# A hybrid SSM and attention layer on one core: VectorE's order up to the scan, with the tables of C A^d built last

## The chip, the cores and the metric

One core of a Trainium2 chip runs the whole layer in one launch. The time is device microseconds from the start to the end of the program, as the median of several runs. The engines meant below are TensorE (PE, with its weight loads PEld), VectorE (DVE), ScalarE (ACT), GpSimd (POOL) and SyncE (SP), whose queue issues nearly all DMAs. Each works through its own list of instructions in order; an instruction that waits on a semaphore holds up all that stand behind it on its engine.

## The reference

One layer of a decoder, in float32, for 1024 positions of 1024 features. What the change touches lies in the first sub-layer, up to the state scan:

```python
mod = (silu(c) @ w_mod + b_mod)                  # sh1, sc1, g1, sh2, sc2, g2
h = _rms(x, norm1_w) * (1 + sc1) + sh1
proj = h @ w_in                                  # u (512) | q (512) | k (128) | v (128)
# S5: 32 groups of 16 channels, each driving a complex state of 64
a = exp(dt * lam); bb = f * (b_re + i b_im)      # zero-order hold
bu = einsum("blgh,gph->blgp", u, bb)
s[t] = a * s[t-1] + bu[t]                        # associative scan over the 1024 positions
y = Re(C s) + D u; z = gelu(y); out = z * sigmoid(z @ w_glu + b_glu)
# beside it: sliding-window attention (128) with sinks on q, k, v; then per-branch norms,
# w_out and the gate g1; then the channel sub-layer: norm, w_up, conv of width 3, silu gate, w_down
```

## The kernel before

A scheduler puts the instructions of each engine in an order when the program is built; the code gives it dependences and priorities. `tc.issue_after(i)` makes what stands inside it come after instruction i in that order. Tiles with one name share one place in SBUF: a new tile of a name may be written once all readers of the old one are done. All products that must be exact run as three products of rounded halves (`mm3`), each half made by a ScalarE cast and a VectorE subtraction (`split`).

**Load stage.** For eight blocks of 128 features, x, one column block of w_mod and the weights of u come in. VectorE makes a column of sc1 (`emit_mod`, L178: a product of 128x1024 with a running sum), scales and splits x into `hT`, and TensorE adds to six banks for u (positions j, j+8, ... for j = 0 to 5) and, through a matrix of ones, the sums of squares in banks 6 and 7. `rsqrt_mean` (L187) makes `rstd` of these, with two ScalarE and two VectorE steps for each half. Then the eight numbers that scale u (`rc`) are turned by TensorE, and the products for j = 6 (in bank 6) and j = 7 (in bank 0) follow.

**Shift.** Eight more `emit_mod` make the columns of sh1 (L291 to L293) from 512 KB blocks that pass through three places. `shs` holds them rounded, `shift_u` (L299) multiplies them with the weights of u on TensorE, and VectorE reduces that to `Bu`.

**Tables.** From A^0 to A^8 (`PWr`, `PWi`) the helper `outer` makes, on VectorE, four tables `IB` of B A^d (128x1024, 8 steps of d) and five tables `CAt` of C A^d (128x1008 and 128x576, 9 steps). Each table takes two products and a sum.

**Up to the scan.** Positions go in 128 chunks of 8. U (in the place S16) is transposed by TensorE, four groups to a bank, and ScalarE adds Bu on the way out (`emit_ut`); the tables IB are transposed too (`emit_wj`, ScalarE copies). Three banks (4, 5, 6) take turns for both. Their product gives what each chunk adds to the states; ScalarE copies it to SR and SI, which lie in S16 as well, so that their first writers (two memsets, L578 and L579) wait until U is transposed. `h0` is a generator that puts the products for the key, value and query heads between these steps; inside `pe.pin(True)` TensorE's order is as written.

**Scan.** `cmac` works up and down six levels on VectorE, through a bank (`bk7`) for the products; eight instructions for each half of the first level, one dependent on the other. The columns of the heads are normed between them. After the scan the halves of SR and SI are exchanged (ScalarE, VectorE, ScalarE), and TensorE makes y with the tables CA; gelu, GLU and attention follow.

Of the kernel before, what the change touches and what calls it, by code (L numbers as in the profile page):

```python
# [14 lines left out]
ADD, SUB, MUL, MAX, MIN = ALU.add, ALU.subtract, ALU.mult, ALU.max, ALU.min  # L15

L = 1024
D = 1024
# [44 lines left out]
def hymba_kernel(ctx, tc, xT, c, wmod, wu, wkvq, small, consts, relb, pq, wglu, wout, wup, wdn, out):  # L63
# [7 lines left out]
    def new(tag, dt=F32):  # L71
        return pool.tile([128, SIZES.get(tag, 1024)], dt, tag=tag, name="t" + tag)
# [44 lines left out]
    def tt(eng, o, a, b, op):  # L117
        return eng.tensor_tensor(out=o, in0=a, in1=b, op=op)  # L118
# [7 lines left out]
    def stt(o, a, s, b, op0, op1):  # L126
        return vec.scalar_tensor_tensor(out=o, in0=a, scalar=s, in1=b, op0=op0, op1=op1)  # L127
# [41 lines left out]
    cact = new("X7")  # L169
# [17 lines left out]
    def rsqrt_mean(o, t_, ps, n):  # L187

        act.activation(out=o, in_=ps, func=AF.Abs_reciprocal_sqrt, scale=1.0 / n, bias=eps)
        act.activation(out=t_, in_=o, func=AF.Square, scale=math.sqrt(0.5 / n))  # L190
        stt(t_, ps, n * 1e-6, t_, ADD, MUL)
        stt(o, t_, -1.5, o, ADD, MUL)

    ab, na = [0], [3]

# [71 lines left out]
    rtmp = new("A11")  # L267
    for h in range(2):
        hs = slice(h * 512, h * 512 + 512)
        rsqrt_mean(rstd[:, hs], rtmp[:, hs], bank[6 + h], D)  # L270
    for j in range(T):
        pe.matmul(bank[7][:, j:j + 1], rstd[0:1, j:1024:T], ones[0:1, 0:1], start=True, stop=True)
    act.copy(rc, bank[7][:, 0:8])
# [14 lines left out]
        u_out(j, b)  # L288


    mst = [new("X4"), new("X5"), new("A9")]  # L291
    for k in range(8):
        emit_mod(k, mst[k % 3], cact)  # L293
    shs = pool.tile([128, 16], F32R, name="shs")
    shr = RT(shs.rearrange("p (k s) -> p k s", s=2))
    act.copy(shr.r[:, :, 0], mod[:, 0:8])
# [2 lines left out]
    def shift_u():  # L299
        b = mbank()  # L300
        for k in range(8):
            s_ = [shs[:, 2 * k + i:2 * k + i + 1].to_broadcast([128, 128]) for i in range(2)]
            pe.matmul(b, s_[0], wus[k][0].r, start=(k == 0), stop=False)
            pe.matmul(b, s_[0], wus[k][1].r, start=False, stop=False)
            pe.matmul(b, s_[1], wus[k][0].r, start=False, stop=(k == 7))
        tmp = new("A11")[:, 0:512]
        tt(vec, gh(tmp), gh(b), S("mod16").rearrange("p (o h) -> p o h", o=1).to_broadcast([128, 32, 16]), MUL)
        vec.tensor_reduce(out=Bu, in_=gh(tmp), axis=mybir.AxisListType.X, op=ADD)

# [105 lines left out]
    def outer(eng, o, tmp, g0, ng, nd, u, v):  # L415
        o = o.rearrange("p (g d h) -> p g d h", d=nd, h=16)
        tmp = tmp.rearrange("p (g d h) -> p g d h", d=nd, h=16)
        shp = [128, ng, nd, 16]

        def bx(w_):  # L420
            return gh(w_)[:, g0:g0 + ng, :].rearrange("p g (o h) -> p g o h", o=1).to_broadcast(shp)

        def by(w_):
            return w_[:, g0:g0 + ng, 0:nd].rearrange("p g (d o) -> p g d o", o=1).to_broadcast(shp)

        tt(eng, o, bx(u), by(PWr), MUL)
        tt(eng, tmp, bx(v), by(PWi), MUL)
        tt(eng, o, o, tmp, ADD)

    IB = [new(f"A{5 + i}") for i in range(4)]  # L430
    hp = ctx.enter_context(ExitStack())
    hp.enter_context(tc.high_priority(0))
    for i in range(4):
        tmp = new("A10") if i == 3 else IB[i + 1]
        outer(vec, IB[i], tmp, 8 * i, 8, 8, Bb, Bsw)
    hp.close()
    CAt = [new(f"A{i}") for i in range(5)]
    for i in range(4):
        outer(vec, CAt[i][:, 0:1008], CAt[i + 1][:, 0:1008], 7 * i, 7, 9, P1, P2)
    for q in range(2):  # L440
        outer(vec, CAt[4][:, q * 288:(q + 1) * 288], CAt[4][:, 600:888], 28 + 2 * q, 2, 9, P1, P2)

    def CA(g):
        return CAt[g // 7][:, (g % 7) * 144:(g % 7 + 1) * 144]


    sA, sB = new("X4"), new("X5")
# [90 lines left out]

    def emit_ut(i):
        if i % 2 == 0:  # L540
            UTt[i // 2] = new(f"A{5 + i // 2}")
        b = abank()
        for q in range(4):
            g = 4 * i + q
            pe.transpose(b[:, q * 128:(q + 1) * 128], U[:, g * 128:(g + 1) * 128], ident)
        for q in range(4):
            g = 4 * i + q
            act.activation(out=UTt[i // 2][:, (g % 8) * 128:(g % 8 + 1) * 128], in_=b[:, q * 128:(q + 1) * 128], func=AF.Identity, bias=Bu[:, g:g + 1])

    for i0, n_ in ((0, 4), (4, 2), (6, 2)):  # L550
        for i in range(i0, i0 + n_):
            emit_wj(i)
        for i in range(i0, i0 + n_):
            emit_ut(i)

    def UT(g):
        return UTt[g // 8][:, (g % 8) * 128:(g % 8 + 1) * 128]
# [7 lines left out]
    for i in range(4):  # L565
        br_, bi_ = abank(), abank()
        for q in range(4):
            for par in range(2):
                g = 2 * (4 * i + q) + par
                ps = slice(par * 64, par * 64 + 64)  # L570
                pe.matmul(br_[ps, q * 128:(q + 1) * 128], WJ(g)[:, 0:64], UT(g), start=True, stop=True)
                pe.matmul(bi_[ps, q * 128:(q + 1) * 128], WJ(g)[:, 64:128], UT(g), start=True, stop=True)
        next(h0)
        evac(SR[:, 4 * i:4 * i + 4, 1:129], br_.rearrange("p (g c) -> p g c", c=128), "I")
        if i != 1:
            next(h0)
        evac(SI[:, 4 * i:4 * i + 4, 1:129], bi_.rearrange("p (g c) -> p g c", c=128), "I")
    vec.memset(SR[:, :, 0:1], 0.0)  # L578
    vec.memset(SI[:, :, 0:1], 0.0)  # L579

    pst.close()


    em, mid = new("A9"), new("A10")
# [780 lines left out]
```

## Time and profile before

| | |
|---|---|
| median of 3 runs | 1137.26 us (1137.13 to 1140.05) |
| the profiled execution | 1138.01 us |
| its span in the trace | 1136.1 us |
| TensorE busy | 92% |
| VectorE busy | 82% |
| ScalarE busy | 51% |
| GpSimd busy | 24% |
| mean granted clock of TensorE | 0.962 |

The span leaves out some 1.9 us of the execution around it. A busy share is a mean over stages with different limits, so the stage from the load to the scan is read by itself, from the order of instructions in time and from what ended each wait. Times in rows are us from the span's start. A row of a timeline gives the start, the busy time of the whole group, the engine, the line, the operation, what it writes and reads, and the count; busy times of neighbours overlap a little, so that the distance from start to start is the step.

### The profile page before, as it was taken

Reading aid. Unit: us, or ns where it says so; the run is one execution under the profiler, and the core shown is the slowest. Engines: PE = TensorE matmul, PEld = TensorE weight load, DVE = VectorE, ACT = ScalarE, POOL = GpSimd, SP = SyncE. Lnnn points to the kernel's source line nnn. Section 1 sums busy time; section 2 is a strip of 40 time slices with the busy share of each in tenths; the row PEclk is TensorE's granted clock in tenths of the full one; section 3 lists DMA queues with packets and bytes.
Section 4 is the critical chain, followed back from the end, with each engine's and each line's share of the span. In section 5 each row is a group of like instructions: output and inputs, shape, how many; then the busy total and the mean of one; then the engine's idle time right before and its main releaser. Section 6 shows DMA issues by size and latency. Waiting matters only on the chain.

```text
span 1136.1 us, 13319 instructions
## 1 busy us (share of the span) xinstructions
PE 1050.8 (92%) x4692; PEld 828.1 (73%) x4692; DVE 928.0 (82%) x1493; ACT 581.0 (51%) x1008; POOL 269.0 (24%) x153
## 2 busy tenths in 40 slices
PE   6989999579989899779999999999999979989998
PEld 4877777366556577657888888888888768768876
DVE  7994899949887587888777878797778797998985
ACT  5415443578895366736544545455444554434342
POOL 0000000011233102762222223212212143353541
PEclk9989999689999899979999999999999989999999
DMA  9501516014018855222223232423123359220002
GB/s 364 224 19 38 118 50 93 1 66 139 19 47 213 258 180 155 93 93 94 92 86 112 82 128 93 154 88 112 56 93 116 125 210 382 74 93 1 1 38 112
DMA packets 48487, 128.14 MB, mean 113 GB/s; under 512 B 6146, under 2 KB 14114, under 8 KB 48419
## 3 DMA queue, kind: packets, MB, share of 16 engines
q1 hardware_dynamic: 46114, 123.09, 31.8%
q0 software_dynamic: 2304, 4.20, 2.3%
q8 instruction: 37, 0.61, 0.2%
q14 instruction: 32, 0.25, 0.1%
HBM read 105.28 MB, written 21.99 MB: 112 GB/s over the span
## 4 chain that ended last, share of the span: by engine, by line
PE 44%; DVE 11%; ACT 1%; DMA 1%; issue 1%; SPq 0%; DVEq 0%; ACTq 0%
PE bk L97 43%; DVE tA L118 2%; DVE tH L118 2%; DVE tU L118 2%; PE bk L99 1%; DVE tXQ L127 1%; DVE tX L127 1%; DVE tXQ L118 1%; DVE tX L118 1%; DVE tS L118 1%; DMA tS<-in_dram 0%; DMA tX<-xd 0%; ACT tU L133 0%; DVE tHA L118 0%; DMA tW<-in_dram 0%
## 5 line engine op out<-in xcount | busy, mean ns | idle before, releaser
L97 PE MATMUL bk<-tA,tU 128*128 128x512 f32 x516 | 128.1, 395 | 0.8 <-DVE tA L118 0.8
L97 PE MATMUL bk<-tU,tU 128*128 128x512 f32 x516 | 123.4, 391 | 4.8 <-DVE tXQ L127 2.4
L97 PEld LDWEIGHTS bk<-tU,tU 128*128 128x128 f32 x516 | 96.5, 188 | 27.4 <-issue 2.8
L97 PE MATMUL bk<-tH,tU 128*128 128x512 f32 x477 | 115.9, 392 | 0.0
L97 PEld LDWEIGHTS bk<-tA,tU 128*128 128x128 f32 x516 | 96.7, 188 | 24.2 <-DVE tA L118 1.4
L127 DVE SCALAR_TENSOR_TENSOR tX<-tH,sm,tX 128x1023 f32<-128x1023 f32 x66 | 100.2, 1519 | 7.7 <-ACT tX L1100 7.6
L97 PEld LDWEIGHTS bk<-tH,tU 128*128 128x128 f32 x477 | 89.1, 188 | 19.2
L97 PE MATMUL bk<-tA,tXQ 128*128 128x512 f32 x300 | 74.5, 395 | 1.0 <-ACT tH L1053 1.0
L97 PE MATMUL bk<-tH,tA 128*128 128x512 f32 (+1 forms) x168 | 62.5, 502 | 10.6 <-ACT tH L133 6.5
L99 PE MATMUL bk<-tH,tU 128*128 128x512 f32 x267 | 65.8, 402 | 2.3 <-DVE tU L118 2.3
L97 PEld LDWEIGHTS bk<-tA,tXQ 128*128 128x128 f32 x300 | 56.3, 188 | 14.5 <-ACT tH L1053 1.4
L133 ACT CAST tU<-tW 128x512 fp32r<-128x512 f32 (+1 forms) x67 | 47.1, 710 | 38.1 <-PE bk L97 19.9
L118 POOL TENSOR_TENSOR tU<-tW,tU 128x512 fp32r<-128x512 f32 x25 | 36.5, 1467 | 115.1 <-ACT tU L133 93.4
L118 DVE TENSOR_TENSOR tX<-tX,tX 128x512 f32<-128x512 f32 (+1 forms) x63 | 61.6, 982 | 1.7 <-DMA tX<-in_dram 0.9
L118 POOL TENSOR_TENSOR tXQ<-tW,tXQ 128x512 fp32r<-128x512 f32 x12 | 49.8, 4154 | 52.3 <-ACT tXQ L133 32.5
L99 PEld LDWEIGHTS bk<-tH,tU 128*128 128x128 f32 x267 | 51.0, 193 | 15.3 <-DVE tU L118 3.1
L118 POOL TENSOR_TENSOR tH<-tH,att 128x1024 f32<-128x1024 f32 (+1 forms) x9 | 17.0, 1890 | 176.2 <-DVE att L841 149.2
L118 POOL TENSOR_TENSOR tU<-tX,tU 128x512 fp32r<-128x512 f32 x19 | 32.9, 1736 | 85.4 <-ACT tU L133 71.3
L118 DVE TENSOR_TENSOR tU<-tW,tU 128x512 fp32r<-128x512 f32 (+2 forms) x43 | 37.8, 881 | 18.2 <-ACT tU L133 18.2
L97 PE MATMUL bk<-tXQ,tH 128*128 128x256 f32 (+2 forms) x224 | 50.2, 368 | 1.6 <-DVE att L829 1.6
L118 DVE TENSOR_TENSOR tU<-tX,tU 128x512 fp32r<-128x512 f32 x39 | 31.3, 808 | 23.4 <-ACT tU L133 23.4
L97 PEld LDWEIGHTS bk<-tXQ,tH 128*128 128x128 f32 x224 | 44.5, 268 | 8.2 <-DVE att L829 4.3
(351 smaller groups left out, 2423.4 us busy)
## 6 DMA issues: line engine op xcount, KB each, us to landing
tW<-in_dram SPq DMA_DIRECT2D x49, 512.0 KB, 3.3
tX<-in_dram SPq DMA_DIRECT2D x47, 512.0 KB, 3.3
tS<-in_dram SPq DMA_DIRECT2D x30, 512.0 KB, 7.1
gd<-tX SPq DMA_DIRECT2D x22, 512.0 KB, 2.9
tA<-in_dram SPq DMA_DIRECT2D x12, 512.0 KB, 10.0
tH<-in_dram SPq DMA_DIRECT2D x12, 512.0 KB, 5.0
tH<-gd SPq DMA_DIRECT2D x8, 512.0 KB, 4.4
tA<-gd SPq DMA_DIRECT2D x8, 512.0 KB, 9.8
```

The lines of the kernel that those rows point to most:

```text
L97: return f(*a, **k)
L99: i = f(*a, **k)
L118: return eng.tensor_tensor(out=o, in0=a, in1=b, op=op)
L127: return vec.scalar_tensor_tensor(out=o, in0=a, scalar=s, in1=b, op0=op0, op1=op1)
L133: act.copy(o, i)
```

## The change

VectorE's four steps of the first norm are marked, and the eight `emit_mod` of the shift and the building of the IB tables are put after them (`issue_after(normed1)`). The third place of the shift's blocks is A4 and no longer A9. The CA tables are built after the last IB table (`issue_after(built)`), in the places A5 to A8 and A4, where the four IB tables lie first; the transposed U goes to A0 to A3. All eight `emit_ut` are put ahead of all eight `emit_wj`, and one step of the heads stands between them.

```diff
-        stt(o, t_, -1.5, o, ADD, MUL)
+        return stt(o, t_, -1.5, o, ADD, MUL)
...
-        rsqrt_mean(rstd[:, hs], rtmp[:, hs], bank[6 + h], D)
+        normed1 = rsqrt_mean(rstd[:, hs], rtmp[:, hs], bank[6 + h], D).ins
...
-    mst = [new("X4"), new("X5"), new("A9")]
-    for k in range(8):
-        emit_mod(k, mst[k % 3], cact)
+    mst = [new("X4"), new("X5"), new("A4")]
+    with tc.issue_after(normed1):
+        for k in range(8):
+            emit_mod(k, mst[k % 3], cact)
...
-        outer(vec, IB[i], tmp, 8 * i, 8, 8, Bb, Bsw)
+        with tc.issue_after(normed1):
+            built = outer(vec, IB[i], tmp, 8 * i, 8, 8, Bb, Bsw)
     hp.close()
-    CAt = [new(f"A{i}") for i in range(5)]
...
-            UTt[i // 2] = new(f"A{5 + i // 2}")
+            UTt[i // 2] = new(f"A{i // 2}")
...
-    for i0, n_ in ((0, 4), (4, 2), (6, 2)):
-        for i in range(i0, i0 + n_):
-            emit_wj(i)
-        for i in range(i0, i0 + n_):
-            emit_ut(i)
+    for i in range(8):
+        emit_ut(i)
+        if i == 3:
+            next(h0)
+    for i in range(8):
+        emit_wj(i)
...
-        next(h0)
+        if i:
+            next(h0)
         evac(SR[:, 4 * i:4 * i + 4, 1:129], br_.rearrange("p (g c) -> p g c", c=128), "I")
...
     pst.close()
+
+    CAt = [new(f"A{i}") for i in (5, 6, 7, 8, 4)]
+    later = ExitStack()
+    later.enter_context(tc.issue_after(built))
+    for i in range(4):
+        outer(vec, CAt[i][:, 0:1008], CAt[i + 1][:, 0:1008], 7 * i, 7, 9, P1, P2)
+    for q in range(2):
+        outer(vec, CAt[4][:, q * 288:(q + 1) * 288], CAt[4][:, 600:888], 28 + 2 * q, 2, 9, P1, P2)
+    later.close()
```

What this makes of the order is seen at three places. In a row a name has the tile's place and a running number (tA5_561 is in A5). The first is VectorE at the end of the load stage, behind the last split of x (tH15_98), before the change: tA5 to tA8 and tA10 hold products for the IB tables, tA0 to tA4 those for the CA tables, the ISA rows are `emit_mod`, tA11_364 and tX6_362 are the norm's steps.

```order
L118 TENSOR_TENSOR tA6_562<-tU4_153,PWi_464 128x1024
L118 TENSOR_TENSOR tA1_579<-tU5_152,PWi_464 128x1008
L118 TENSOR_TENSOR tA2_580<-tU5_152,PWi_464 128x1008
L118 TENSOR_TENSOR tA7_563<-tU4_153,PWi_464 128x1024
L118 TENSOR_TENSOR tA3_581<-tU5_152,PWi_464 128x1008
L118 TENSOR_TENSOR tA8_564<-tU4_153,PWi_464 128x1024
L118 TENSOR_TENSOR tA10_574<-tU4_153,PWi_464 128x1024
L118 TENSOR_TENSOR tA4_582<-tU5_152,PWi_464 128x1008
L652 COPY ep_1445<-PWi_464 64x16 x2
L180 ISA tX5_440,mod_80<-tX5_440,tX7_75,sm_71 128x1024
L180 ISA mod_80 128x1
L127 SCALAR_TENSOR_TENSOR tA11_364<-bk6_69,tA11_364 128x512
```

The same place after it:

```order
L127 SCALAR_TENSOR_TENSOR tH15_98<-tS16_74,mods_81,tH14_97 128x1024
L118 TENSOR_TENSOR ep_1445<-ep_1445 128x16 x20
L127 SCALAR_TENSOR_TENSOR tA11_364<-bk6_69,tA11_364 128x512
L127 SCALAR_TENSOR_TENSOR tX6_362<-tA11_364,tX6_362 128x512
L127 SCALAR_TENSOR_TENSOR tA11_364<-bk7_70,tA11_364 128x512
L127 SCALAR_TENSOR_TENSOR tX6_362<-tA11_364,tX6_362 128x512
L180 ISA tX4_439,mod_80<-tX4_439,tX7_75,sm_71 128x1024
L180 ISA mod_80 128x1
L180 ISA tX5_440,mod_80<-tX5_440,tX7_75,sm_71 128x1024
```

The eight products and the block of the shift that stood between the last split and the norm are gone from there; the scan's powers (ep) stand there instead, and the norm's four steps are together.

The second place is VectorE between the shift and the scan. tU3_1002 is a split of a head's weights, Bu the shift's sum, the memsets the first writers of the scan's tile in S16. Before:

```order
L118 TENSOR_TENSOR tU3_1002<-tW0_999,tU2_1001 128x1024
L118 TENSOR_TENSOR tA4_582<-tU5_152,PWi_464 128x288
L118 TENSOR_TENSOR ep_1445<-ep_1445 128x16
L118 TENSOR_TENSOR tA4_582<-tA4_582 128x288
L118 TENSOR_TENSOR ep_1445<-ep_1445 128x16 x12
L578 MEMSET tS16_774 128x16
L579 MEMSET tS16_774 128x16
L118 TENSOR_TENSOR bk7_70<-tS16_774,ep_1445 128x512
L118 TENSOR_TENSOR tS16_774<-tS16_774,bk7_70 128x8x64
```

After (tA5_847 to tA8_850 are CA tables in the places of the IB tables):

```order
L309 TENSOR_REDUCE Bu_82<-tA9_611 128x32
L468 COPY bcol_585<-bk6_69 128x1
L574 MEMSET tS16_754 128x16
L575 MEMSET tS16_754 128x16
L118 TENSOR_TENSOR tA5_847<-tU5_152,PWr_463 128x1008
L118 TENSOR_TENSOR tA6_848<-tU5_152,PWi_464 128x1008
L118 TENSOR_TENSOR tA7_849<-tU5_152,PWi_464 128x1008
L118 TENSOR_TENSOR tA5_847<-tA5_847,tA6_848 128x1008
L118 TENSOR_TENSOR tA8_850<-tU5_152,PWi_464 128x1008
L118 TENSOR_TENSOR tA6_848<-tU5_152,PWr_463 128x1008
L118 TENSOR_TENSOR tA6_848<-tA6_848,tA7_849 128x1008
L118 TENSOR_TENSOR tA7_849<-tU5_152,PWr_463 128x1008
```

The CA tables moved from ahead of the memsets to behind them; the scan's first product follows the last row shown, and the rest of the tables stands between the scan's first instructions.

The third place is TensorE behind the shift. tS16 rows are transposes of U, tA5 to tA8 rows those of IB, tU2_1001 and tU3_1002 the two halves of a head's weights. Before:

```order
L99 MATMUL bk4_67<-cn_73,tA5_561 128x128 x4
L97 MATMUL bk6_69<-cn_73,brow_609 128x1
L99 MATMUL bk5_68<-cn_73,tA5_561 128x128 x4
L97 MATMUL bk1_64<-tHA_85,tU2_1001 128x512 x2
L99 MATMUL bk6_69<-cn_73,tA6_562 128x128 x4
L99 MATMUL bk4_67<-cn_73,tA6_562 128x128 x4
L99 MATMUL bk5_68<-cn_73,tS16_382 128x128 x4
L97 MATMUL bk1_64<-tHA_85,tU3_1002 128x512
```

After (the head's products run on from the second row for 21 in all, and the next transposes of U come behind them):

```order
L99 MATMUL bk4_67<-cn_73,tS16_382 128x128 x4
L97 MATMUL bk1_64<-tHA_85,tU2_1001 128x512 x2
L97 MATMUL bk1_64<-tHA_85,tU3_1002 128x512
L97 MATMUL bk1_64<-tHB_86,tU2_1001 128x512 x2
L97 MATMUL bk1_64<-tHB_86,tU3_1002 128x512
...
L97 MATMUL bk1_64<-tH12_95,tU3_1002 128x512
L97 MATMUL bk6_69<-cn_73,brow_586 128x1
L99 MATMUL bk5_68<-cn_73,tS16_382 128x128 x4
```

The transposes of the IB tables, which came first, now come last, behind all those of U. On TensorE the turning of rstd moved too, from behind the products for j = 6 to their middle, and the squares of the last feature block moved from 36 to 18 products ahead of the end of the load stage. After the scan the list of VectorE has the second exchange copy behind two more score evaluations of the attention than before.

## Rows read from the trace of the kernel before

**Rows 1.** The page's first part: busy us, share of the span, instructions of each engine.
```profile
PE 1050.8 (92%) x4692; PEld 828.1 (73%) x4692; DVE 928.0 (82%) x1493; ACT 581.0 (51%) x1008; POOL 269.0 (24%) x153
```

**Rows 2.** Busy time by stretch. Columns: stretch and its length, then busy us (and instructions) of PE, PEld, DVE, ACT and POOL, the granted clock of TensorE, the DMA engines' share, GB/s.
```profile
62.10:66.50 4.40, 0.00 (x0) 0.00 (x0) 4.35 (x8) 0.00 (x0) 0.00 (x0) 1.00 0.00 0
66.50:70.00 3.50, 3.46 (x8) 2.84 (x9) 3.50 (x5) 0.00 (x0) 0.00 (x0) 0.52 0.48 150
78.00:82.00 4.00, 3.02 (x8) 2.50 (x8) 3.75 (x6) 3.17 (x6) 0.00 (x0) 0.50 0.00 0
99.80:116.70 16.90, 15.20 (x130) 11.99 (x128) 0.10 (x2) 10.98 (x36) 0.32 (x2) 1.00 0.08 12
129.60:234.00 104.40, 91.23 (x465) 70.05 (x458) 100.58 (x199) 47.87 (x72) 0.00 (x0) 0.90 0.30 59
```

**Rows 3.** What VectorE waited for between 20 and 129.6 us: who waited, for whom, us in total, times, the longest.
```profile
DVE tS L578 <- PE bk L99: 10.0, 1, 10.0
DVE bk L118 <- ACT tS L133: 7.3, 2, 6.8
DVE tA L118 <- PE bk L99: 1.3, 1, 1.3
DVE tU L118 <- ACT tU L133: 1.1, 1, 1.1
DVE tS L122 <- ACT rc L273: 0.4, 1, 0.4
```

**Rows 4.** VectorE's timeline in the load stage and behind it (CUSTOM_DVE_ANT_0 is `emit_mod`).
```profile
24.07 1.28 DVE L180 CUSTOM_DVE_ANT_0 tA<-tA,tX,sm 128x1024 f32<-128x1024 f32 x1
...
55.20 9.10 DVE L118 TENSOR_TENSOR tA<-tU,PWi 128x1024 f32<-128x1024 f32 x8
64.22 0.34 DVE L652 COPY ep<-PWi 64x16 f32<-64x16 f32 x2
64.59 1.28 DVE L180 CUSTOM_DVE_ANT_0 tX<-tX,tX,sm 128x1024 f32<-128x1024 f32 x1
...
65.80 1.28 DVE L127 SCALAR_TENSOR_TENSOR tA<-bk,tA 128x512 f32<-128x512 f32 x2
...
72.89 1.28 DVE L180 CUSTOM_DVE_ANT_0 tX<-tX,tX,sm 128x1024 f32<-128x1024 f32 x1
```

**Rows 5.** TensorE's timeline from the end of the load stage to the shift, and one group of the products for the states.
```profile
52.70 9.38 PE L97 MATMUL bk<-tXQ,tH 128*128 128x512 f32 x36
66.54 1.67 PE L97 MATMUL bk<-tU,tHA 128*128 128x512 f32 x3 [4.47 <-DVE tA L127]
...
74.05 3.96 PE L97 MATMUL bk<-cn,tX 1*128 1x1 f32 x16
78.99 1.67 PE L97 MATMUL bk<-tU,tHA 128*128 128x512 f32 x3 [0.97 <-ACT tS L279]
...
86.89 2.94 PE L99 MATMUL bk<-tU,shs 128*128 128x512 f32 x12
...
92.45 1.12 PE L99 MATMUL bk<-tU,shs 128*2 128x128 f32 x16
...
114.08 2.02 PE L99 MATMUL bk<-tA,tA 128*64 128x128 f32 x32
```

**Rows 6.** VectorE's timeline from the shift's product to the end of the scan's first level.
```profile
92.65 0.69 DVE L118 TENSOR_TENSOR tA<-bk,sm 128x512 f32<-128x512 f32 x1 [1.27 <-PE bk L99]
...
94.65 0.66 DVE L308 TENSOR_REDUCE Bu<-tA 128x32 f32<-128x512 f32 x1
...
97.75 2.05 DVE L118 TENSOR_TENSOR ep<-ep 128x16 f32<-128x16 f32 x12
109.80 0.07 DVE L578 MEMSET tS<- 128x16 f32 x1 [10.00 <-PE bk L99]
...
116.71 0.70 DVE L118 TENSOR_TENSOR bk<-tS,ep 128x512 f32<-128x512 f32 x1 [6.81 <-ACT tS L133]
117.44 0.69 DVE L118 TENSOR_TENSOR tS<-tS,bk 128x512 f32<-128x512 f32 x1
...
128.85 0.72 DVE L118 TENSOR_TENSOR tS<-tS,bk 128x512 f32<-128x512 f32 x1
```

**Rows 7.** ScalarE's timeline: the norm's table load and steps, the transposed U with Bu (L548), the copies of the transposed tables, and the first copies to SR and SI.
```profile
52.67 1.28 ACT L189 ACT_TABLE_LOAD   x1 [1.30 <-DVE tH L127]
53.96 1.27 ACT L189 ACTIVATE tX<-bk,sm 128x512 f32<-128x512 f32 x2
55.12 1.15 ACT L190 ACTIVATE tA<-tX 128x512 f32<-128x512 f32 x2
...
102.27 3.21 ACT L548 ACTIVATE tA<-bk,Bu 128x128 f32<-128x128 f32 x12 [3.31 <-PE bk L99]
105.29 1.16 ACT L133 COPY tA<-bk 128x512 f32<-128x512 f32 x2
106.23 2.29 ACT L548 ACTIVATE tA<-bk,Bu 128x128 f32<-128x128 f32 x8
...
112.44 1.08 ACT L133 COPY tS<-bk 128x512 f32<-128x512 f32 x2 [0.87 <-PE bk L99]
```

**Rows 8.** DMAs of weights to tW in 25 to 200 us: us from issue to landing.
```profile
DMA to landing us min/median/max: 3.2/3.3/7.5
```

**Rows 9.** VectorE's second exchange copy behind the scan.
```profile
232.54 0.69 DVE L710 COPY tS<-tS 64x1024 f32<-64x1024 f32 x1
```

More of the change, by code (lines that the diff above doesn't have):

```diff
@@ L305, in shift_u @@
             pe.matmul(b, s_[1], wus[k][0].r, start=False, stop=(k == 7))
-        tmp = new("A11")[:, 0:512]
+        tmp = new("A9")[:, 0:512]
         tt(vec, gh(tmp), gh(b), S("mod16").rearrange("p (o h) -> p o h", o=1).to_broadcast([128, 32, 16]), MUL)
@@ L427, in outer @@
         tt(eng, tmp, bx(v), by(PWi), MUL)
-        tt(eng, o, o, tmp, ADD)
+        return tt(eng, o, o, tmp, ADD).ins
     IB = [new(f"A{5 + i}") for i in range(4)]
@@ L434, in hymba_kernel @@
         tmp = new("A10") if i == 3 else IB[i + 1]
-        outer(vec, IB[i], tmp, 8 * i, 8, 8, Bb, Bsw)
+        with tc.issue_after(normed1):
+            built = outer(vec, IB[i], tmp, 8 * i, 8, 8, Bb, Bsw)
     hp.close()
-    CAt = [new(f"A{i}") for i in range(5)]
[L438 to L444, printed above, removed]
     sA, sB = new("X4"), new("X5")
@@ L581, in hymba_kernel, with CA @@
     pst.close()
+    CAt = [new(f"A{i}") for i in (5, 6, 7, 8, 4)]
[6 more added lines that the diff above has]
+    later.close()
+    def CA(g):
+        return CAt[g // 7][:, (g % 7) * 144:(g % 7 + 1) * 144]
     em, mid = new("A9"), new("A10")
```

## The prediction

> **What bounds the kernel now.** The page's busy shares come first: TensorE is busy for 92% of the span and VectorE for 82% [rows 1], which would make TensorE the bound of the whole. The change lies in one stage, so I read the busy times by stretch next, and there it is otherwise. From 129.6 to 234 us VectorE is busy for 100.58 of 104.4 us, TensorE for 91.23 at a mean granted clock of 0.90 [rows 2]. So the scan and the heads' norms are VectorE's time: whatever moves VectorE's end of the scan's first level moves the stretch up to the second exchange copy at 232.54 [rows 9], and y, gelu and the attention's exponentials come behind that copy. Third, the list of VectorE's waits: up to the end of the first level (128.85 + 0.72 = 129.57 us, [rows 6]) it waits 10.0 + 7.3 + 1.3 + 1.1 + 0.4 = 20.1 us in all [rows 3], and 10.0 and 6.8 of that lie in one gap from 99.8 to 116.7 us, where it waits for U's transposes and then for the first copies to SR [rows 2, 6]. The timelines then give the chain in front of that gap. TensorE runs its 36 last products of the load stage to 62.08 us, sits idle for 4.47 us because bank 6 is still to be read by the norm's first VectorE step, which stands behind eight table products and a column of the shift, and goes on at 66.54 [rows 4, 5].
>
> The change therefore comes down to an account of one engine. VectorE's instructions are the same in kind and number before and after, so up to the first level's end its time is the same work plus its waits. I work out the new waits, and the difference from 20.1 us is the answer.
>
> **Load stage.** TensorE has no gap between the products before 62.08 [rows 5], so I keep that end. The last squares now stand 18 products ahead of it: 18 x 0.26 (9.38 / 36) = 4.7 us, so they are done at 57.4, their bank 6 half about 0.9 earlier, at 56.5. ScalarE then loads its table (1.28 us) and makes two steps of some 0.6 us for each half [rows 7]. VectorE's first norm step can start at 59.2 and the fourth ends at about 61.8; before, the norm began at 65.80 [rows 4] and its last step ended near 71.8. TensorE's bank 6 is free at 59.9, so its 4.47 us wait goes.
> VectorE, though, gives up work that filled its time. From 24.07 to 65.80 it had 41.7 us without a gap. Out of this go six columns of the shift at 1.2 us (64.59 to 65.80), ten table products at 1.13 us (9.0 / 8): 7.2 + 11.3 = 18.5 us. In come about 20 small instructions of the scan's powers at 0.17 us (2.05 / 12, [rows 6]), some 3 us. It is done at 24.07 + 41.7 - 18.5 + 3 = 50.3, and waits until 59.2: **8.9 us**, and 0.2 between the steps.
>
> **Shift.** From 61.8 VectorE has a full list up to Bu: eight columns (9.6), nine IB steps before the last column and `shs` and four after it, with one CA product (14 x 1.13 = 15.8), two scalings of u (1.3), two splits of weights (2.3), and the shift's product, sum and small copies (1.5): 30.5 at most, 29.3 where neighbours overlap. The blocks' loads are reissued at 62.9, 64.1 and 65.3 and, at 3.3 us [rows 8], lie ready before their turn. `shs` is ready at 81.8 (before, about 76.5), and TensorE, done with j = 7 at about 78, waits some 3 to 4 us for it. The shift's product ends near 88.5 (before: 92.45), and Bu is ready at 91.7 with 0.6 us of waits, against 95.3 before [rows 6]. So TensorE's saved 4.47 and 0.97 us [rows 5] turn into a wait for `shs`, and 3.6 us are left.
> [...]
> [...]
>
> **Up to the scan.** All eight transposed U come first now, but the second of them stands on TensorE behind 21 products of a head. Their weights come into W0 after the split at 85.2, land at 88.6 [rows 8], and are cast and split by 90.9; 20 products x 0.25 and four transposes end at 96.4. From there ScalarE sets the pace: 1.0 us for four pieces (3.02 / 3 from 102.27 to 105.29, [rows 7]), so the last U is out at 103.5 and the eight table copies at some 0.5 us (two from 105.29 to 106.23) follow to 107.5. VectorE's memset waits until about 101.1 for the last transposes of U, and the first CA table, whose place A5 is the first IB table's, until that has been transposed at 103.1. So from 91.7 VectorE has 0.2 us to do and waits **11.2 us**. A memset ahead of the tables in the order costs nothing more, since A5 comes free later still.
> The four places A5 to A8 come free about 1.0 us apart, VectorE takes 1.13 us a step, and waits 0.2. The states' product takes 2.0 us [rows 5]; the first four copies to SR and SI are done at 112.8, against 116.7 before. VectorE has by then done eight steps of the tables (9.0 of 14.6 us; the last six short steps are 0.37 each, 128x288 against 128x1008), waits 0.5 for the scan's first product and makes the other 5.6 us between the scan's first instructions.
>
> **Sum.** New waits: 8.9 + 0.2 + 0.6 + 11.2 + 0.7 = 21.6 us against 20.1: the first level ends 1.5 us later, 131.1 us. Behind it VectorE waits 3.8 us at most in 104 [rows 2], so nothing takes this up. The second exchange copy stands behind two more score evaluations, 0.6 us. 1138.01 + 1.5 + 0.6 = 1140.1 us for the profiled execution; that one lies 0.75 us above the median of its runs, so **1139.4 us** against 1137.26, or +0.2%.
> Bounds. The waits of the load stage lie between 7.5 (the squares done 1.4 us sooner) and 10.5 us (ScalarE's steps ending later by the 1.3 us between its starts, rows 7, and a little more). The gap in front of the tables lies between 7.4 (the head's products not in the way, 3.8 us less) and 15.4 us (the weights landing after 7.5 and not 3.3 us, [rows 8]). What the scheduler ordered differently behind 240 us no row prices; I allow 2 us on both sides, some three of VectorE's 0.7 us steps there.
>
> **Rivals.**
> *Slower: the head's weights come late.* One late split holds 21 products, behind them seven transposes of U, the eight of the tables, and so both the scan's data and the places of the tables. Each us of landing above 3.3 is one us of the end; from 4.6 us on it passes 0.3% with the 2.1 us above. For it: the slowest landing is 7.5 us, and the products could also run at the lower clock behind TensorE's wait (0.43 and not 0.26 us each, 20 x 0.17 = 3.4 us). Against: nothing else is on the DMA queues at that time, and the median is 3.3. Time: 1139.4 + 3.4 to 4.2, about 1143.
> *Faster: the 3.6 us at Bu get through.* If U's second transposes do not wait (split early, or norm steps early enough), the chain from Bu to the scan is 3.8 us shorter, the first CA step starts at 99.3, and the first level ends at 127.3: -2.3, with the copy's 0.6 still to pay; with the load stage at its lower bound -1.4 more and interleaved tables that cover the steps between dependent scan instructions (0.73 from start to start, 117.44 - 116.71) half a us more. About -3.6: 1133.7. For it: the old gap of 16.9 us is the largest single one [rows 2]. Against: TensorE's order shows the head's products in between.
> *TensorE decides.* If it were TensorE that bounds the stretch, its 4.47 + 0.97 us and the half clock of 66.5 to 70 and 78 to 82 us would be the gain: 5.4 + 1.4 + 1.3 = 8.1, so 1129. Against it stand VectorE's 100.58 of 104.4 us.
> *Nothing moves but the order.* The tables only change places within VectorE's waits, and the end of the scan is unmoved: 1137.3. It falls into the same class as my forecast.
>
> **Chances.** About 0.3% (3.4 us) is what a measurement of this kernel can tell from no change. My forecast, with the unmoved end, has 0.48 and by itself a range of 1134 to 1140.6. Late weights and other losses that add up behind the scan have 0.31; the gain that gets through has 0.16, and TensorE as the bound 0.05. So faster 0.21, same 0.48, slower 0.31. The range that should hold 8 in 10 reaches from the lower rival's surroundings to past the upper one: 1132 to 1145 us.
>
> **What would show it.** In the profile after, TensorE goes on at 62 us without the 4.47 us wait, and has a wait of 3 to 4 us for `shs` in front of the shift's product; VectorE shows about 9 us idle ahead of the first norm step and one of about 11 us in front of the memset and the first CA product; Bu is ready at 91 to 92 us; the first copies to SR start near 109; the second exchange copy is at 234 to 236. I am wrong if the idle time ahead of the norm is under 5 us, if the CA products start before 100 us, or if the copy moves by more than 3 us from 234.6.

## The result and the profile after

The kernel after takes 1145.22 us (median of 6 runs, 1142.96 to 1147.51) against 1137.20 us of six runs before (1134.13 to 1140.05): a ratio of 1.0084, interval 1.0066 to 1.0102. It is slower by 8.0 us between these medians, and by 9.6 us by the ratio. The prediction was 1139.4 us with a range up to 1145.0. One run below, of the kernel after with a second place for weights, took 4834.69 us and is not in its ratio. The profiled execution took 1143.18 us, its span is 1141.4 us, and the mean granted clock of TensorE is 0.959 (before 0.962).

The page's busy times are those of before to within 0.3% for the two engines that carry the kernel [rows 1], so most of the lost time is waiting:

```profile
PE 1052.9 (92%) x4692; PEld 826.8 (72%) x4692; DVE 928.6 (81%) x1493; ACT 582.7 (51%) x1008; POOL 271.5 (24%) x153
```

VectorE's waits from 20 us to the end of the scan's first level, columns as in [rows 3]:

```profile
DVE tA L127 <- ACT tA L190: 7.6, 1, 7.6
DVE tS L574 <- PE bk L99: 5.6, 1, 5.6
DVE bcol L468 <- PE bk L97: 4.2, 1, 4.2
DVE tA L118 <- PE bk L99: 2.2, 2, 1.9
DVE tU L118 <- ACT tU L133: 0.3, 1, 0.3
DVE tX L127 <- ACT tX L190: 0.2, 1, 0.2
```

They make 20.1 us, as before. The first row is the idle time ahead of the norm, the next two and 1.9 of the fourth are the gap in front of the CA tables. VectorE's timeline puts them in time, to compare with [rows 4, 6, 9]:

```profile
58.99 0.69 DVE L127 SCALAR_TENSOR_TENSOR tA<-bk,tA 128x512 f32<-128x512 f32 x1 [7.57 <-ACT tA L190]
...
91.20 0.67 DVE L309 TENSOR_REDUCE Bu<-tA 128x32 f32<-128x512 f32 x1
...
103.82 1.21 DVE L118 TENSOR_TENSOR tA<-tU,PWr 128x1008 f32<-128x1008 f32 x1 [1.91 <-PE bk L99]
...
131.97 0.68 DVE L118 TENSOR_TENSOR tS<-tS,bk 128x512 f32<-128x512 f32 x1
...
233.17 0.69 DVE L718 COPY tS<-tS 64x1024 f32<-64x1024 f32 x1
```

At the second exchange copy the kernel after is 0.6 us late against [rows 9] (1.9 us in a second profile, 234.48). The rest is lost behind it, in the 100 us in which the attention runs beside GLU. TensorE's timeline there; a bracket is the wait ahead of the row and what ended it:

```profile
61.33 0.88 PE L97 MATMUL bk<-tU,tHA 128*128 128x512 f32 x3
...
80.94 0.73 PE L99 MATMUL bk<-tU,shs 128*128 128x512 f32 x2 [1.01 <-ACT shs L297]
...
92.17 3.57 PE L97 MATMUL bk<-tH,tU 128*128 128x512 f32 x15
...
316.00 1.23 PE L97 MATMUL bk<-tXQ,tH 128*128 128x256 f32 x4 [4.25 <-DVE att L837]
...
341.38 4.61 PE L97 MATMUL bk<-tA,tHB 128*128 128x512 f32 x12 [3.20 <-DVE tA L127]
```

The last two waits make 7.45 us together. The longest that before has from 300 to 350 us are 1.67 and 1.61 us, at 314.87 and 322.48. TensorE is busy for 41.54 us there, and was for 45.82 before: 4.3 us less. Busy time by stretch, columns as in [rows 2], of the kernel after:

```profile
300.00:350.00 50.00, 41.54 (x170) 23.65 (x170) 40.95 (x116) 44.96 (x120) 11.49 (x7) 0.90 0.08 23
```

and of before:

```profile
300.00:350.00 50.00, 45.82 (x205) 28.77 (x205) 42.01 (x122) 47.36 (x126) 15.00 (x9) 0.97 0.28 82
```

The DMA share fell too, from 0.28 to 0.08. The reload of c (`cad`) and the blocks of the last modulation go into S16, where z lies until GLU's last split has read it. SyncE's queue issues c first and the first block right behind it (at 354.90 after, 341.55 before). After:

```profile
354.51 0.34 SPq L902 DMA_DIRECT2D tS<-cad  x1
```

Before:

```profile
341.16 0.34 SPq L894 DMA_DIRECT2D tS<-cad  x1
```

VectorE's list says what TensorE waits for at 312 us. `att L837` are the score evaluations of an attention unit, and `tA<-tS,tA` are the splits of z for GLU:

```profile
308.45 1.86 DVE L122 TENSOR_SCALAR att<-att 128x4 f32<-128x4 f32 x1
...
310.38 4.16 DVE L118 TENSOR_TENSOR tA<-tS,tA 128x512 fp32r<-128x512 f32 x4
314.46 0.68 DVE L127 SCALAR_TENSOR_TENSOR tS<-tU,tS 128x512 f32<-128x512 f32 x1
315.06 0.47 DVE L837 CUSTOM_DVE_ANT_0 tA<-bk,tA,sm 128x256 f32<-128x256 f32 x1
```

The same work in a second profile of before:

```profile
310.74 0.68 DVE L118 TENSOR_TENSOR tA<-tS,tA 128x512 fp32r<-128x512 f32 x1
311.34 0.47 DVE L829 CUSTOM_DVE_ANT_0 tH<-bk,tA,sm 128x256 f32<-128x256 f32 x1
...
312.15 1.88 DVE L118 TENSOR_TENSOR tA<-tS,tA 128x512 fp32r<-128x512 f32 x3
```

Before, two evaluations stand between the first split and the other three; after, all four splits and one more step stand ahead of the unit's evaluations, for 4.7 us (310.38 to 315.06). The scheduler made another plan of this stage, 200 us behind the edit. Of VectorE's 368 instructions from 236 to 430 us in before, only 191 stand in the same order in after (counted by line, operation, size and names).

### The profile page after: what moved, and what is told of

Its sections match the earlier page's. It is cut to its first block, busy times and chain, and to the rows that moved or that the text cites. A ratio compares the mean times of both kernels' runs of the same rounds, so it can differ in the third digit from the quotient of the medians.

```text
span 1141.4 us, 13314 instructions
## 1 busy us (share of the span) xinstructions
PE 1052.9 (92%) x4692; PEld 826.8 (72%) x4692; DVE 928.6 (81%) x1493; ACT 582.7 (51%) x1008; POOL 271.5 (24%) x153
## 4 chain that ended last, share of the span: by engine, by line
PE 59%; DVE 24%; DMA 7%; ACT 6%; issue 3%; POOL 1%; SPq 0%; ACTq 0%; DVEq 0%; POOLq 0%
PE bk L97 55%; DVE tA L118 4%; PE bk L99 4%; DMA tW<-in_dram 3%; DVE tU L118 3%; DVE tH L118 3%; DVE tX L127 2%; DMA tS<-in_dram 2%; DVE tS L118 2%; DVE bk L118 2%; ACT tU L133 1%; DVE tX L118 1%; ACT tH L846 1%; DVE tXQ L118 1%; DMA cn<-in_dram 1%
## 5 line engine op out<-in xcount | busy, mean ns | idle before, releaser
L97 PE MATMUL bk<-tXQ,tH 128*128 128x256 f32 (+2 forms) x224 | 55.3, 390 | 7.0 <-DVE att L837 7.0
```

Of the source, the lines that this page charges most:

```text
L97: return f(*a, **k)
```

## The experiments

Theory A is that this order behind the scan costs most of the time; its rivals put the loss into the front, or into one named step. Medians of before on the same chips were 1135.3 to 1136.4 us. "Copy" is the start of the second exchange copy (it stands behind different work in the two plans, and so is a rough mark), "c" the reload of c, and "TensorE" its busy time from 300 to 350 us, all in us of one profile each.

| kernel | ratio to before (95%) | copy | c | TensorE |
|---|---|---|---|---|
| before, again | 0.9997 (0.9983 to 1.0010) | 232.76 | 341.45 | 45.86 |
| after, again | 1.0082 (1.0068 to 1.0097) | 234.48 | 356.53 | 41.54 |
| after, a copy on VectorE | 1.0031 (1.0019 to 1.0043) | 235.46 | 345.37 | 45.48 |
| before, a copy on VectorE | 1.0007 (0.9996 to 1.0019) | 234.38 | 343.03 | 45.49 |
| tables last alone | 1.0052 (1.0033 to 1.0071) | 229.29 | 351.19 | 41.48 |
| tables last, a copy on VectorE | 0.9994 (0.9984 to 1.0003) | 230.26 | 341.14 | 45.83 |
| norm first alone | 1.0088 (1.0068 to 1.0108) | 237.19 | 357.92 | 41.40 |

**GLU's late splits, in the kernel before.** The four splits of GLU's second half are put behind the attention's unit 14, the order that the kernel after has for them.

```diff
-            split(mx[n, h], src)
+            if h == 0:
+                split(mx[n, h], src)
...
+    with tc.issue_after(unit[14]):
+        for n in range(4):
+            split(mx[n, 1], zT[n][:, 512:1024])
```

> The kernel before, unchanged up to the scan, with the last four splits of GLU's second half put behind the 15th attention unit. Theory A (the loss lies behind the scan: the tile S16 comes free later, so the loads of the last 16 modulation blocks and the output weights start later and TensorE waits for them): the load of c at 341.2 us moves to about 350 us, and the time rises by 3 to 6 us, to 1140 to 1143 us. Theory B (the loss comes from the order up to the scan): no change, 1136 to 1138 us.

Measured 1142.99 us, ratio 1.0058 (1.0037 to 1.0079), with the front as before (copy at 231.98) and the reload of c at 348.17, the blocks right behind it. Late splits, with the loads that wait for them, cost some 6.6 us: theory A holds so far. TensorE has none of the two long waits of after here (busy for 44.89 us from 300 to 350), so an order can cost this much without them.

**GLU first, in the kernel after.** Unit 16's evaluations and unit 15's scalings are put behind GLU's last split.

```diff
+            glu_done = split(mx[n, h], src).ins
...
+                    with (tc.issue_after(glu_done) if u > 14 else ExitStack()):
```

> The changed kernel with the last attention unit's evaluations and the 15th unit's scalings put behind GLU's last split, as they stand in the kernel before. Theory A: the load of c comes before 345 us (354.5 in the changed kernel), and the time falls by 3 to 6 us, to 1139 to 1142 us. Theory B: 1144 to 1147 us, as the changed kernel.

A miss: 1145.15 us, 1.0087 (1.0066 to 1.0108). The reload of c came 3.5 us sooner (351.02), but the attention's last unit ended at 364.15 and not 353.7, and the waits of 4.25 and 3.19 us stayed. One stage forward puts the other back.

**Tables last without norm first.** Both `issue_after(normed1)` are undone.

> The changed kernel without the two waits on the norm: the shift's columns and the IB tables may stand ahead of the norm's steps again; behind the scan its order is nearly that of the changed kernel. Theory A: TensorE has its 4.5 us wait at 62 us again, VectorE loses its 7.6 us idle time there, the second exchange copy moves by under 3 us, and the time stays at 1142 to 1148 us. Theory B: with the norm's steps late again most of the loss goes: 1137 to 1140 us.

1140.69 us, 1.0052. TensorE had no 4.5 us wait (it goes on at 61.58), and the copy came 3.9 us sooner than after, at 229.29; both were expected otherwise. So the two `issue_after(normed1)` are not needed for TensorE's wait to vanish: with the CA tables out of the load stage the norm's first step comes at 60.12 by itself.

**Norm first without tables last**, the other half, on the kernel before.

> The kernel before with the two waits on the norm alone (tables, U and heads in the old order). VectorE idles some 5 to 8 us ahead of the norm's first step, TensorE has no 4.5 us wait at 62 us, and Bu comes at 91 to 92 us. If the norm's steps first cost 3.9 us in front of the scan in either order of the tables, the second exchange copy comes at 234 to 237 us (232.5 in the kernel before); if the loss needs the tables last as well, at 231 to 233 us. Behind the scan the order differs from both kernels, so the whole time is between 0 and 8 us above the kernel before.

1145.71 us, 1.0088, copy at 237.19. TensorE's timeline shows the price; `shs` closes the columns of the shift:

```profile
86.21 1.22 PE L99 MATMUL bk<-tU,shs 128*128 128x512 f32 x2 [5.78 <-ACT shs L297]
88.40 4.64 PE L99 MATMUL bk<-tU,shs 128*128 128x512 f32 x10 [0.97 <-DVE shs L118]
```

The columns now come behind the norm, and beside them VectorE still builds both kinds of tables, so TensorE waits 6.75 us for `shs`. Bu is made at 100.03 us, against 94.65 [rows 6] and 91 to 92 expected, and the whole chain to the scan follows 5.4 us later:

```profile
100.03 0.67 DVE L309 TENSOR_REDUCE Bu<-tA 128x32 f32<-128x512 f32 x1
```

Against 232.5 before, tables last moves the copy by -3.3 us, norm first by +4.7, and both by +0.6 (233.17) to +2.0 (234.48).

**The head's step behind the transposes**, undoing `if i == 3: next(h0)` and `if i:`.

> The changed kernel with the head's 21 products back behind the first of the states' products, so that all transposes of U come directly one behind the other. The first CA product starts at 99 to 100 us (103.8 in the changed kernel) and the scan's first level ends 2 to 4 us earlier. Behind the scan the order is nearly that of the kernel before. Theory A: GLU's last splits come by 345 us, and the time is 1133 to 1138 us. Theory B (only the products' 3.8 us count): 1141 to 1142 us.

1145.18 us, 1.0085, the first CA product at 105.19 and not 103.82. The edit moved only 3 of the products; the others stand between U's transposes by the scheduler's choice, so it did not test what it was meant to.

**One copy on another engine, to bring the old plan back.** The list of engines for the copies to SR and SI is `a` (ScalarE); its eighth entry becomes VectorE. With this the scheduler's order behind the scan is that of before: of the 368 instructions of VectorE counted above, 360 stand in the same order. Inside the scan the edit also moves some steps of the heads' norms, from 125 us on.

```diff
-    "EI": "a",
+    "EI": "aaaaaaav",
```

> The changed kernel with one of its eight copies to SR and SI (the last) on VectorE instead of ScalarE. Up to the scan nothing else moves; behind the second exchange copy the order on all engines becomes that of the kernel before, but for some rows next to that copy. Theory A2 (what costs the time is the order of attention and GLU that the scheduler made behind the scan, in 300 to 410 us): the second exchange copy stays within 1.5 us of the changed kernel's 233.2, the load of c comes at 341 to 344 us, and the time falls by 3.5 to 6 us against the changed kernel, to within 0.3% of the kernel before. Theory B (the order up to the scan costs it): 0 to 1 us slower than the changed kernel.

1138.39 us, 1.0031, just outside the 0.3% expected, although the copy at 235.46 is 1 us later than in the second profile of after. What moved inside the scan has thus gained nothing by the copy. The control is the same edit in before, where the order behind the scan does not change:

> The kernel before with the same copy to SR and SI on VectorE as in e5_copy_dve; the order behind the scan stays that of the kernel before. If the copy itself is worth nothing, as theory A2 needs: ratio 0.999 to 1.002, and e5_copy_dve gained by the order alone. If the copy on VectorE is a gain of its own: 3 to 6 us faster than the kernel before.

1136.60 us, 1.0007: the edit makes the copy 1.6 us late (234.38 against 232.76), but is worth nothing at the end. So the plan behind the scan costs 0.0082 - 0.0031 = 0.0051, 5.8 us (by the two intervals about 2 us either way), and the front some 3 us. The 5.8 us are a net figure. ScalarE's first table load behind gelu comes sooner with the plan of after, the slow plan (the first row, from its second profile), than with the old plan (the second row, from this run):

```profile
243.53 1.28 ACT L844 ACT_TABLE_LOAD   x1
...
246.44 1.28 ACT L844 ACT_TABLE_LOAD   x1
```

There the slow plan is 2.9 us ahead, and behind it it loses that and 5.8 us more. Part of the 2.9 us is the edit's own: the control has this load at 243.22, and before at 241.26 and 241.51, 1.7 us that do not reach the control's end. So behind gelu the slow plan loses some 7 to 9 us, an estimate. The timeline of TensorE has no wait over 1.7 us from 305 to 345 us here, and the busy time is back:

```profile
300.00:350.00 50.00, 45.48 (x207) 28.36 (x206) 43.77 (x128) 46.63 (x118) 14.85 (x8) 0.97 0.22 56
```

**Tables last with the old plan.** The copy on VectorE is the fifth of the list.

> The changed kernel without the two waits on the norm (as e3_norm_late) and with the fifth copy to SR and SI on VectorE, which brings back the order of the kernel before behind the scan. Theory A2: the two parts add up, 3.2 us from the front of e3_norm_late (second exchange copy at 229 to 230 us) and no loss behind it: 2.5 to 3.5 us faster than the kernel before (ratio 0.997 to 0.998). Theory B: as e3_norm_late, some 5 us slower than the kernel before.

1135.04 us, 0.9994 (0.9984 to 1.0003); 0.997 to 0.998 was expected. The plan's loss is gone again (1.0052 without it), but the front's gain does not arrive: 2.5 us at the copy (230.26 against 232.76) are 0.4 us by ScalarE's table load behind gelu (241.09 against 241.51). What takes them back is not shown. Tables last alone, with the slow plan, has its table load at 238.20, so there the gain of 3.1 us does reach this point, and is lost behind it.

**Both kernels again**, for the spread of their profiles.

> The changed kernel itself, beside the others on one chip: 7 to 10 us slower than the kernel before. Its second profile shows what repeats: the second exchange copy within 1.5 us of 233.2, the load of c near 354 us.

> The kernel before itself: ratio 0.998 to 1.002. Its second profile shows how far one profiled execution stands for the others: the profiles of e5 to e8 lie 2 to 4 us nearer to the first profile of the kernel before than their medians do, so the first profile should be a slow one; expected here is a span 1 to 3 us shorter (1133 to 1135 us), with the time lost in the first profile somewhere behind the second exchange copy.

Both are in the table. The second profile of before has a span of 1131.5 us, shorter than expected; it is taken up at the end.

**Which step of the plan costs it.** Four single steps were put late, or made longer, in the kernel before. The reload of c behind unit 14, and behind unit 15:

```diff
+    with tc.issue_after(unit[14]):
+        vec.memset(cact3[:, 0:1], 0.0)
```

> The kernel before with one small memset on VectorE behind the 15th attention unit, which the load of c into S16 waits for; GLU and its splits stay where they are. The load of c comes at 347 to 349 us (341 before). Theory A3 (the loads are the gate): as e1_glu_late, 5 to 7 us slower than the kernel before (ratio 1.004 to 1.006). Rival (GLU's own late splits are the gate): within 1 us of the kernel before.

> The same, held until the 16th unit: the load of c at 355 to 360 us. Theory A3: 9 to 12 us slower than the kernel before (ratio 1.008 to 1.0105), as the changed kernel. Rival: within 1 us.

The reload moved to 347.65 and 351.57 (355 to 360 expected for the second), and the ratios are 1.0010 (0.9998 to 1.0023) and 0.9999 (0.9986 to 1.0012). SyncE's queue in the second, where `tS<-in_dram` are the blocks of the modulation:

```profile
341.01 1.37 SPq L179 DMA_DIRECT2D tS<-in_dram  x3
351.57 0.33 SPq L896 DMA_DIRECT2D tS<-cad  x1
357.45 2.74 SPq L179 DMA_DIRECT2D tS<-in_dram  x3
```

Ten us of delay of c alone cost nothing. The edit does not hold the blocks: three go out at 341 us as in before, while none goes out ahead of 354.90 in after. So that all these loads come late, the most visible shift of the profile after, stays untested as a cause by itself. The second load of the output weights, whose place W0 is taken late, behind unit 9:

> The kernel before with one small memset on VectorE into W0 behind the tenth attention unit, so that the second load of output weights starts at 317 to 320 us as in the changed kernel (308.7 before), and with it all later loads through W0. Theory A5 (the chain of loads through W0 is the gate): 4 to 8 us slower than the kernel before (ratio 1.0035 to 1.007). If the chain has that much slack: within 1.5 us.

1138.25 us, 1.0016 (1.0002 to 1.0029): 1.8 us for a load 7.5 us later (316.16 against 308.70), less than theory A5 needs. And 17 products more on TensorE ahead of a projection of GLU's output, 17 x 0.24 = 4.1 us by this row of its timeline (12 products stood there, and 29 do now):

```profile
343.20 6.95 PE L97 MATMUL bk<-tA,tHA 128*128 128x512 f32 x29
```

> The kernel before with 17 products more (0.25 us each, 4.2 us in all, each written over by the next) ahead of the seventh output block's first product, at 340 to 350 us. Theory A6 (TensorE is the bound from 300 to 430 us, and each us it loses in waits there is lost): 3 to 5 us slower than the kernel before (ratio 1.0026 to 1.0044). If TensorE has slack there: under 1.5 us.

1139.97 us, 1.0027 (1.0016 to 1.0039): 3.1 of the 4.1 us reach the end (1.8 to 4.4 by the interval). Here TensorE is nearly the bound. At the same share its 4.3 us less of busy time by 350 us would be worth 3.2, an estimate.

**A second place for the output weights.** The first four blocks alternate between W0 and W1 and no longer share W0.

```diff
-        st = new("W0" if i < 4 else f"W{i % 2}")
+        st = new(f"W{i % 2}")
```

On tables last with the old plan, on the kernel after, and on before:

> The kernel of e6_norm_late_copy_dve with the output weights of the attention branch loaded in turn into W0 and W1, and not the first four all into W0. If the weights' chain (load, cast, split, next load, some 6 us each) is what TensorE waits for in 385 to 410 us, 1 to 4 us faster than the kernel before (ratio 0.9965 to 0.999), the fastest kernel of this study; if the shared DMA queues alone limit it, as e6, 0.999 to 1.000.

> The changed kernel with the output weights of the attention branch loaded in turn into W0 and W1. If the weights' chain is what TensorE waits for in 385 to 410 us, 2 to 4 us faster than the changed kernel (1141 to 1143 us beside a kernel before at 1136); if the shared DMA queues alone limit it, no change.

> The kernel before with the output weights of the attention branch loaded in turn into W0 and W1, as in e13_two_places, and nothing else. If that place is the whole gain of e13: 0.995 to 0.998. If e13 needed the tables last as well: 0.999 to 1.001.

1131.11 us (0.9964, 0.9949 to 0.9980), 1142.04 us (1.0049, 1.0030 to 1.0068) and 1133.25 us (0.9973, 0.9960 to 0.9986): some 3 us in each. So these loads do not tell after from before; the gain is the place's own. The first of the three beats both kernels, and so does the last, by so little less that the intervals overlap. In the first profile of before the loads of two of these blocks went out at

```profile
365.40 0.38 SPq L901 DMA_DIRECT2D tW<-in_dram  x1
...
380.83 0.38 SPq L872 DMA_DIRECT2D tW<-in_dram  x1
```

They went out at 361.95 and 376.91 in its second profile, and with two places in before at

```profile
363.12 0.38 SPq L901 DMA_DIRECT2D tW<-in_dram  x1
...
366.06 0.38 SPq L872 DMA_DIRECT2D tW<-in_dram  x1
```

## Why the prediction was wrong, point by point

- **Load stage**: right. TensorE goes on at 61.33 us (62 forecast), and VectorE idles for 7.57 us ahead of the norm (8.9; bounds 7.5 to 10.5).
- **Shift**: right in its end, wrong in one wait. `shs` is read from 80.9 to 81.9 us (81.8) and Bu is made from 91.20 (ready at 91.7 forecast), but TensorE waits 1.01 + 0.25 us for it and not 3 to 4, since it came there about 2 us later than I took. The 0.6 us of VectorE's own waits ahead of Bu no run shows: it waits 0.30 us there, for the cast of a head's weights, and TensorE runs the shift's product at a granted clock of 1.00 (80.94 to 88.08).
- **Up to the scan**: right in the waits, 1.6 us short at the end. The gap in front of the CA tables is 4.22 + 5.57 + 1.91 = 11.7 us (11.2); the first CA product starts at 103.82 (103.1). The waits add up to 20.1 us and not 21.6. The first level nevertheless ends at 131.97 + 0.68 = 132.65 (131.1), mostly because three more steps of the heads' norms, some 2.1 us, were put ahead of its end. That is moved work, and the copy at 233.17 and 234.48 lies at the forecast 234.6 or below it.
- **Sum**: the step that failed is "What the scheduler ordered differently behind 240 us no row prices; I allow 2 us on both sides". It had no row behind it, and it is 5.8 us, shown by the kernel after with the old plan (1.0031 against 1.0082) and a second time, as 6.6 us, by tables last (0.9994 against 1.0052). Nor are "some three of VectorE's 0.7 us steps" what it consists of: the order of the whole stage changed, and TensorE waits. With the old plan the front's +2.1 us would have been near the mark: some 3 us were measured. In the kernel after itself the first table load behind gelu is only 0.5 and 2.0 us late (241.80 and 243.53, against 241.26 and 241.51), so most of the loss arises behind gelu.
- **Slower: the head's weights come late.** Its time of 1143 was near by luck, its mechanism did not occur: the 15 products in the row at 92.17 take 0.24 us each (3.57 / 15) at a granted clock of 1.00, without a wait over 1.2 us. The 0.43 us of the prediction is 3.46 / 8 behind TensorE's wait before, at 0.52 [rows 2].
- **Faster: the 3.6 us at Bu get through.** It did not: Bu is made 3.45 us sooner (91.20 against 94.65), but the head's products stand in the way, as the prediction's objection said, and the copy is late.
- **TensorE decides.** Wrong up to the scan: TensorE goes on 5.2 us sooner (61.33 against 66.54), and the copy comes no sooner. Of its 1.4 us, 3.46 - 8 x 0.26 at a granted clock of 0.52 [rows 2], nothing is left on TensorE: the 12 products from 61.33 take 2.93 us, 0.24 each, at 1.00. The granted clock of 0.50 in 78 to 82 us [rows 2] is there still, only sooner: 0.50 in 70 to 74 us, where the seven products at 69.45 take 3.38 us, 0.48 each. Behind 300 us it is nearly true, and I had not asked it of that stretch.

Shown is that the plan of the attention and GLU costs the 5.8 us, and that late splits of GLU, with the loads behind them, cost as much in the kernel before. The two TensorE waits of 4.2 to 4.3 and 3.0 to 3.2 us are in every kernel with the slow plan (after, GLU first, tables last alone, norm first alone, the head's step, after with two places) and in none of the others. How the 5.8 us divide between these waits, the late splits and the later loads stays open; no run holds the loads alone. So does why the scheduler chooses this plan; I only found an edit that makes it choose the other.

## What to carry to other kernels

Where a scheduler plans the whole program, an edit in one stage plans later ones anew. Compare the order of those later stages as closely as that of the edited one, and price a difference there by the engine that bounds that stretch, never by a small allowance. To split a loss, find an edit without a price of its own that brings the old plan back (here one copy on another engine), with the same edit in the kernel before as the control; and build each half of a change alone, since here one half gained 3.3 us at the copy and the other lost 4.7.

## What the runs showed of the hardware

**Three slow scalings on VectorE end with a product of GpSimd.** A scaling of 128x4 numbers takes VectorE 0.16 us in general and 1.86 us at 308.45 in the kernel after. GpSimd's timeline beside it:

```profile
308.12 2.17 POOL L118 TENSOR_TENSOR tA<-tA,att 128x1024 f32<-128x1024 f32 x1 [10.89 <-DVE att L849]
310.63 2.16 POOL L118 TENSOR_TENSOR tH<-tH,att 128x1024 f32<-128x1024 f32 x1 [0.35 <-DVE att L849]
```

GpSimd's first product ends at 310.29, VectorE's scaling at 310.31. The four splits behind it take 4.16 us, where three take 1.88 before (0.63 each): 4.16 - 4 x 0.63 = 1.6 us more, beside a second product that ends at 312.79. Not every instruction of VectorE takes longer there: in the kernel after an evaluation takes 0.47 us at 323.47, beside GpSimd's product of 321.59 to 323.75, and 0.48 us at 300.26, where GpSimd is idle. What makes the scaling longer no run here shows. The plan of before has such scalings too: one of 1.05 us at 309.40 and one of 1.85 us at 317.90, ending 0.03 and 0.02 us behind a product of GpSimd (307.73 + 2.69 and 317.57 + 2.16). So they are not shown to set the plans apart.

**One stretch sets two profiles of one kernel apart.** The two profiles of the kernel before agree to 0.3 us up to 350 us and differ by some 8 us at 400; 4.6 us of that are left at the end (spans of 1136.1 and 1131.5). In between 16 blocks of modulation weights and the output weights come in. From 380 to 400 us the first profile has

```profile
380.00:400.00 20.00, 14.55 (x50) 11.07 (x49) 12.77 (x24) 7.54 (x11) 1.72 (x2) 0.83 0.71 212
```

and the second

```profile
380.00:400.00 20.00, 17.60 (x74) 13.68 (x75) 15.76 (x29) 10.89 (x15) 1.71 (x2) 1.00 0.72 222
```

with 3 us more of TensorE's work at the full granted clock. The order is the same in both, and in 350 to 380 us the DMA engines are busy for 0.90 and 0.99 of the time, so the loads are the likely cause; what sets the two apart was not tried. Single runs of before lie between 1132.2 and 1140.5 us and say little about a change of 2 us; only medians of many do.
